# Attention scores: the low queries' product with 64 rows alone, both components as row tiles, one maximum per component

## The chip, the core and the metric

The kernel runs on one core of a Trainium2 chip. The core has a matrix engine (TensorE, PE, with weight loads listed as PEld), three engines for elementwise work (VectorE or DVE, ScalarE or ACT, GpSimd or POOL), a queue that issues DMAs (SyncE, SP), an on-chip memory of 128 partitions, and PSUM, the memory into which PE writes, in 8 banks of 512 fp32 columns. Each engine takes its instructions in the order of the program and waits for the others by semaphores. The metric is the device time of one execution in microseconds (us).

## What is computed

One layer of a backbone with two branches on 1024 latent tokens and 256 context tokens, of width 1024: gated linear attention, and differential attention with 8 heads. The change lies in the differential attention. Its core in the reference:

```python
def diff_attention(q1, q2, k1, k2, v, lam):
    ...
    def one_block(qs):
        qb1, qb2 = qs
        s1 = jnp.einsum('bhqd,bhkd->bhqk', qb1, k1).astype(jnp.float32) * scale
        s2 = jnp.einsum('bhqd,bhkd->bhqk', qb2, k2).astype(jnp.float32) * scale
        a = jax.nn.softmax(s1, axis=-1) - lam * jax.nn.softmax(s2, axis=-1)
        return jnp.einsum('bhqk,bhkv->bhqv', a.astype(v.dtype), v)
```

Each head has two components (q1 with k1, q2 with k2) of 64 channels. Every block of 128 queries is scored against 1280 keys (256 of the context, 1024 latent), in both components; each gets a softmax, and their difference multiplies the values.

## The kernel before

**Numbers in two parts.** Matrix products run on fp32r operands, each value split into a high part and a low part (the rest). A product of two values is made of high x high, high x low and low x high. For the scores, where a component has only 64 channels, the kernel stacks the parts on the 128 rows: the key tile `K[comp]` holds the high part of the keys on rows 0-63 and the low part on rows 64-127 (`att_keys`, L1746 and L1747), and the query tile `Q[comp]` holds the same query part on both halves of the rows, `Q[comp][:, 0]` the high one, `Q[comp][:, 1]` the low one. A score bank is thus two products: j = 0 gives high queries x (high + low keys), j = 1 gives low queries x (high + low keys).

**A unit.** `att_scores` walks over 8 heads and 8 query tiles of 128: 64 units. The scores of a unit, 2 x 1280 columns, fill five PSUM banks side by side (`s5`). Banks 0 and 1 hold 1024 columns of component 0 (MAIN), banks 3 and 4 those of component 1, and bank 2 holds the last 256 columns of component 0 beside the first 256 of component 1 (TAIL). A unit makes 8 products of 512 columns (2 components x 2 banks x j) and 4 of 256 columns. There is one set of these banks: `acq("s0")`, `acq("s1")` and `acq("st")` wait until the exponentials of the unit before have read component 0, component 1, and both.

**What follows a unit.** DVE takes the maximum over component 0's 1024 columns, over the tails of both (one instruction, two results), and over component 1's 1024 columns (`att_max`), and a minimum of two negated maxima for each component (`att_exp`). ACT then makes the exponential of 1280 columns with its sum, for each component. `att_mix` (DVE) joins both components: a reciprocal, a factor, and one pass over 1280 columns. `att_tr` transposes the result on PE, ACT, POOL and DVE split it into two parts (`att_split`), `att_av` multiplies it with the values, and `att_fin` normalises, gates and stores the head's output to `d_bT`.

**The order on each engine.** It is made when the program is built, by a planner (`Driver`): tasks are generators that yield a due time or an event, each instruction gets a modelled cost, and the task with the smallest priority number that is due goes next. The scores have priority 0, the transposes 1, A·V 2, and maxima and exponentials -3. `fill` has priority 9: the projections of the merge gates and of both branches (tiles `mb` while the scores' banks are open, `mc` afterwards), which don't depend on the attention until the branch of the attention itself (`d_bT`) comes up. So fill takes the PE time that the attention leaves, as far as the planner's costs tell it. `mm` (L334) gives the planner the cost of a product; `banked` declares which instructions touch the same banks, so that others don't wait for each other.

Of the kernel before, what the change touches and what calls it, by code (L numbers as in the profile page):

```python
# [13 lines left out]
AF = mybir.ActivationFunctionType  # L14
ALU = mybir.AluOpType
AX = mybir.AxisListType
# [4 lines left out]
P = 128  # L21
# [3 lines left out]
T = S + CTX  # L25
# [203 lines left out]
class Hybrid:  # L229
# [20 lines left out]
        mm=("psA", 3), tp=("psA", 2), edge=("sbE", 1), gs=("psA1", 1), go=("psA1", 1), gt=("psA1", 1),  # L250
# [80 lines left out]
            yield  # L331
        self.d.spawn(later(), AtPE(at), prio=-9)

    def mm(self, out, lhsT, rhs, start, stop, more=False):  # L334
        self.ins = self.nc.tensor.matmul(out, lhsT, rhs, start=start, stop=stop, skip_group_check=more).ins  # L335
        n = rhs.free_size()
        c = 0.009 + max(n, 230) * 0.000428 if rhs.dtype == F32R else 0.006 + max(4 * n, 470) / 2400
        return self.d.op("PE", c, [out], [lhsT, rhs])

# [1387 lines left out]
    def att_keys(self):  # L1727

        for hd in range(8):
            c, x = hd // 4, hd % 4  # L1730
            for i in range(10):
                yield self.ev_st["dk", c, i]
            if hd:
                yield self.ev_q[0, 1]
            else:
                yield self.gla_free[3]
                yield from self.acq("hc", 16)
                Driver.places = (T, 2 * T, 3 * T)
                self.hk = self.t("hk", [P, HK], F32R)
            K = []  # L1740
            for comp in range(2):
                rows = slice(64 * comp, 64 * comp + 64)
                yield from self.acq("kk")
                m = (2 * hd + comp) % 3
                kt = self.hk[:, m * T:(m + 1) * T]
                self.dma(kt[0:64], self.d_kT[0][c][x, rows])  # L1746
                self.dma(kt[64:128], self.d_kT[1][c][x, rows])  # L1747
                K.append(kt)
            self.K[hd] = K
            self.d.set(self.ev_k[hd], self.d.when(*K))  # L1750
# [33 lines left out]
    def att_scores(self):  # L1784

        nc, d = self.nc, self.d
        yield self.ev_b
        s5 = self.t("s5", [P, 2 * T])
        for hd in range(8):
            for qt in range(8):  # L1790
                pr, qs = qt // 2, slice((qt % 2) * P, (qt % 2) * P + P)
                yield self.ev_k[hd]
                yield self.ev_q[hd, pr]
                K, Q = self.K[hd], self.Q[hd, pr]

                def score(po, comp, o, n):
                    bank = po.offset % (2 * T) // 512
                    for j in range(2):
                        e = self.mm(po, Q[comp][:, j, qs], K[comp][:, o:o + n], j == 0, j == 1)
                        self.banked(self.ins, "PE", bank)  # L1800
                    return e

                u = dict(hd=hd, qt=qt, E=[None, None], mt=self.t("sm", [P, 2]), mx=[self.t("sm", [P, 1]) for _ in range(2)],
                         z=self.t("sm", [P, 2]), left=2, ev=[Event() for _ in range(3)])

                for comp in range(2):
                    yield from self.acq(f"s{comp}")
                    pm = s5[:, 1536 * comp:1536 * comp + 1024]
                    for x, (o, n) in enumerate(self.MAIN[comp]):
                        e = score(pm[:, x * 512:(x + 1) * 512], comp, o, n)  # L1810
                        if x == 0:
                            yield AtPE(0)
                    d.spawn(self.att_max(u["ev"][comp], u["mx"][comp], pm, 3 * comp, 3 * comp + 1), On(e, "DVE"), prio=-3)
                    yield AtPE(0)
                    if comp == 0:
                        yield from self.acq("st")
                        pt = s5[:, 1024:1536].rearrange("p (c k) -> p c k", c=2)
                        for x in range(2):
                            e = score(pt[:, x], x, *self.TAIL[x])
                        d.spawn(self.att_max(u["ev"][2], u["mt"], pt, 2), On(e, "DVE"), prio=-3)  # L1820
                    elif qt == 7:
                        self.rel("kk", e, 2)
                    d.spawn(self.att_exp(u, comp, s5), On(e, "DVE"), prio=-3)
                    yield AtPE(0)
                if qt % 2 == 1:
                    self.rel("aq", e, 2)
                d.set(self.ev_u[8 * hd + qt])

    def att_max(self, ev, mx, pm, *banks):
        self.dve.tensor_reduce(mx, pm, AX.X, ALU.max, negate=True)  # L1830
        self.banked(self.dve.ins, "DVE", *banks)
        self.d.set(ev)
        return
        yield

    def att_exp(self, u, comp, s5):
        d, mx = self.d, u["mx"][comp]
        yield u["ev"][2]
        yield u["ev"][comp]
        yield d.on("DVE", mx)  # L1840
        self.dve.tensor_scalar(mx, mx, u["mt"][:, comp:comp + 1], None, ALU.min)
        yield from self.acq("e5")
        E = u["E"][comp] = self.t("e5", [P, T])
        yield d.on("ACT", mx)
        e = self.act.activation(E, s5[:, 1280 * comp:1280 * comp + T], AF.Exp, bias=mx, accum_out=u["z"][:, comp:comp + 1])
        self.banked(self.act.ins, "ACT", *range(2 * comp, 2 * comp + 3))
        self.rel(f"s{comp}", e)
        u["left"] -= 1
        if u["left"] == 0:
            self.rel("st", e)  # L1850
            if (u["hd"], u["qt"]) == (7, 7):
                d.set(self.ev_s2)
            d.spawn(self.att_mix(u), On(e, "DVE"), prio=self.PM)
# [610 lines left out]
```

## Time and profile before

| | us |
|---|---|
| runs, median of 3 | 1687.13 (1684.58, 1687.13, 1691.38) |
| span of the profiled execution, from its first instruction to its last | 1685.9 |
| first score product to last | 911.3 to 1438.6 |
| mean clock granted to PE, as a share of the full one | 0.994 |

The span lies 1.2 us under the median of the runs, and within their spread. In the profile's rows an engine stands ahead of its line, operation and tiles ("out<-in"); tile names lose their numbers, so `s` is the scores' banks `s5`, `hk` the keys, `aq` the queries, `e` the exponentials, `at` the transposed and split weights, `vv` the values, `b` the two banks shared by transposes and A·V, `sm` the small statistics. All products have line L335 (in `mm`), all transposes L361, all elementwise work L197 (in a helper). A row of a group ends with its count, its busy time with the mean length of one in ns, and the idle time of the engine ahead of it with what ended it. A row of the timeline begins with its start and its length in us. A row of the table of stretches gives the stretch, its length, then the busy time and the number of instructions on PE, PEld, DVE, ACT and POOL, the granted clock, the DMA share and GB/s.

### The profile page before, as it was taken

The page shows a single profiled execution, that of the slowest core. Times are in us where ns is not written, and L with a number is a line of the kernel's source. Part 1 is how long each engine was busy: PE and PEld are TensorE (multiplying, and loading weights), DVE is VectorE, ACT ScalarE, POOL GpSimd, SP SyncE. Part 2 cuts the span into 40 slices and gives each one's busy share as a digit, 9 for nine tenths or more (in the row PEclk, how much of TensorE's full clock was granted, in tenths as well). Part 3 has the DMA queues.
Part 4 walks back from the last instruction along what each step waited for, and adds up shares of the span by engine and source line. Part 5 has one row for each costly group of instructions (what it writes and reads, how often), then busy time and mean ns, then how long its engine had stood idle before and what let it go on. Part 6 is the DMA issues. An engine that isn't in the chain of part 4 may idle for free.

```text
span 1685.9 us, 24403 instructions
## 1 busy us (share of the span) xinstructions
PE 1641.8 (97%) x8389; PEld 1358.3 (81%) x8389; DVE 1167.5 (69%) x2035; ACT 788.4 (47%) x1624; POOL 601.7 (36%) x649
## 2 busy tenths in 40 slices
PE   8999999999999999999999999999999999999999
PEld 3788788888788888888878888888888787887887
DVE  4797853455578697687762988787787887525694
ACT  4666423343334535455442665556666555411231
POOL 1500200000156475465530446555565555700000
PEclk9999999999999999999999999999999999999999
DMA  8557947687683665645375344345368552279422
GB/s 305 167 205 258 325 164 248 226 282 273 200 258 114 197 203 169 207 134 169 117 196 154 85 128 132 104 116 138 113 169 245 167 157 67 98 234 337 151 100 75
DMA packets 255884, 302.84 MB, mean 180 GB/s; under 512 B 21480, under 2 KB 173968, under 8 KB 255760
## 3 DMA queue, kind: packets, MB, share of 16 engines
q1 hardware_dynamic: 255760, 301.29, 56.9%
q8 instruction: 66, 1.08, 0.3%
q14 instruction: 58, 0.48, 0.1%
HBM read 203.71 MB, written 97.52 MB: 179 GB/s over the span
## 4 chain that ended last, share of the span: by engine, by line
PE 43%; DVE 6%; ACT 2%; DMA 2%; POOL 2%; issue 2%; ACTq 0%; DVEq 0%; POOLq 0%; SPq 0%
PE mc L335 10%; PE mm L335 7%; PE mb L335 7%; PE s L335 6%; PE b L335 5%; DVE sm L197 3%; PE b L361 3%; POOL at L197 2%; DVE e L197 2%; PE go L335 1%; ACT e L197 1%; DMA h<-d_bT 1%; PE mz L335 1%; PE gs L335 1%; PE tp L361 1%
## 5 line engine op out<-in xcount | busy, mean ns | idle before, releaser
L335 PE MATMUL mm<-w,h 128*128 128x512 f32 x1260 | 319.3, 402 | 0.6 <-DVE w L197 0.4
L335 PEld LDWEIGHTS mm<-w,h 128*128 128x128 f32 x1260 | 232.0, 189 | 48.0 <-issue 1.0
L197 DVE TENSOR_REDUCE sm<-s 128x1 f32<-128x1024 f32 (+1 forms) x192 | 194.4, 1037 | 49.0 <-PE s L335 47.4
L335 PE MATMUL mb<-h,wt 128*128 128x512 f32 x744 | 204.5, 407 | 2.5 <-ACT ft L197 2.1
L197 ACT ACTIVATE e<-s,sm 128x1280 f32<-128x1280 f32 x128 | 169.9, 1330 | 68.0 <-DVE sm L197 60.3
L197 POOL TENSOR_TENSOR at<-ac,at 128x512 fp32r<-128x512 f32 x128 | 184.7, 1443 | 10.7
L197 POOL TENSOR_SCALAR at<-ac 128x512 fp32r<-128x512 f32 x128 | 100.6, 786 | 236.0 <-ACT ac L197 166.9
L335 PE MATMUL s<-hk,aq 128*128 128x512 f32 (+1 forms) x768 | 178.2, 365 | 3.2 <-ACT e L197 1.1
L335 PEld LDWEIGHTS mb<-h,wt 128*128 128x128 f32 x744 | 131.1, 190 | 25.9 <-ACT ft L197 3.6
L335 PE MATMUL mc<-h,wt 128*128 128x512 f32 x600 | 141.2, 392 | 1.7 <-DMA h<-d_bT 0.8
L335 PE MATMUL mm<-h,w 128*128 128x512 f32 x576 | 139.4, 398 | 2.7 <-ACT p L197 1.1
L335 PEld LDWEIGHTS s<-hk,aq 128*128 128x128 f32 x768 | 122.3, 190 | 23.9 <-ACT e L197 5.1
L335 PEld LDWEIGHTS mc<-h,wt 128*128 128x128 f32 x600 | 111.3, 188 | 26.9 <-DMA h<-d_bT 3.3
L335 PE MATMUL b<-at,vv 128*128 128x256 f32 x960 | 130.6, 285 | 0.5 <-POOL at L197 0.4
L335 PEld LDWEIGHTS mm<-h,w 128*128 128x128 f32 x576 | 108.6, 191 | 27.0 <-DVE h L197 1.4
L335 PEld LDWEIGHTS b<-at,vv 128*128 128x128 f32 x960 | 122.7, 190 | 5.6 <-POOL at L197 1.2
L197 POOL TENSOR_TENSOR sm<-sm,nhalf 128x2 f32<-128x2 f32 (+2 forms) x94 | 106.1, 1129 | 53.6 <-DVE sm L197 48.1
L197 DVE TENSOR_TENSOR w<-raw,w 128x512 fp32r<-128x512 f32 x120 | 92.5, 789 | 31.5 <-ACT w L197 30.3
L197 ACT ACTIVATE ac<-b 128x512 f32<-128x512 f32 x120 | 71.1, 600 | 84.9 <-PE b L361 79.7
L197 DVE SCALAR_TENSOR_TENSOR e<-e,sm,e 128x1280 f32<-128x1280 f32 x64 | 108.7, 1698 | 0.6
L197 ACT ACTIVATE w<-raw 128x512 fp32r<-128x512 f32 x120 | 72.5, 628 | 70.3 <-DVE raw L197 22.8
L361 PE MATMUL b<-ident,e 128*128 128x128 f32 x598 | 92.5, 276 | 12.4 <-DVE at L197 4.3
(283 smaller groups left out, 2832.5 us busy)
## 6 DMA issues: line engine op xcount, KB each, us to landing
raw<-in_w_in SPq DMA_DIRECT2D x63, 512.0 KB, 4.7
g<-d_s SPq DMA_DIRECT2D x32, 640.0 KB, 5.2
aq<-d_qT SPq DMA_DIRECT2D x128, 128.0 KB, 3.4
d_dv<-pl SPq DMA_DIRECT2D x40, 256.0 KB, 2.2
gv<-d_v SPq DMA_DIRECT2D x40, 256.0 KB, 3.2
d_kT<-pl SPq DMA_DIRECT2D x40, 256.0 KB, 3.0
hk<-d_kT SPq DMA_DIRECT2D x32, 320.0 KB, 5.7
vv<-d_dv SPq DMA_DIRECT2D x16, 640.0 KB, 6.2
```

The source lines that it names most:

```text
L197: self.ins = f(out, *args, **kw).ins
L335: self.ins = self.nc.tensor.matmul(out, lhsT, rhs, start=start, stop=stop, skip_group_check=more).ins
L361: self.nc.tensor.transpose(out, src, self.ident[:n, :n])
```

## The change

The low queries (j = 1) of the four MAIN banks are multiplied with the high keys alone, on 64 rows: rows 0-63 for component 0 and rows 64-127 for component 1. For that, component 1's key tile has its halves swapped, so that its high part lies on rows 64-127. The product of low queries and low keys is thus left out there; the tails keep it. The four products of 64 rows stand at the end of a unit, in pairs of the two components, each into its own bank, after all products of 128 rows. Their cost to the planner is that of half the columns (`share=0.5`). One maximum over all 1280 columns of a component takes the place of its two maxima and the minimum; both maxima are issued after the last product of the unit. Component 1's `s1` and `st` are now both acquired ahead of the tails.

```diff
-    def mm(self, out, lhsT, rhs, start, stop, more=False):
+    def mm(self, out, lhsT, rhs, start, stop, more=False, share=1.0):
...
-        n = rhs.free_size()
+        n = rhs.free_size() * share
...
-                self.dma(kt[0:64], self.d_kT[0][c][x, rows])
-                self.dma(kt[64:128], self.d_kT[1][c][x, rows])
+                for j in range(2):
+                    self.dma(kt[64 * j:64 * j + 64], self.d_kT[j ^ comp][c][x, rows])
...
-                def score(po, comp, o, n):
-                    bank = po.offset % (2 * T) // 512
-                    for j in range(2):
-                        e = self.mm(po, Q[comp][:, j, qs], K[comp][:, o:o + n], j == 0, j == 1)
-                        self.banked(self.ins, "PE", bank)
+                def full(po, comp, o, n, j, start, stop):
+                    e = self.mm(po, Q[comp][:, j, qs], K[comp][:, o:o + n], start, stop)
+                    self.banked(self.ins, "PE", po.offset % (2 * T) // 512)
                     return e
+                def half(po, comp, o, n):
+                    r = slice(64 * comp, 64 * comp + 64)
+                    e = self.mm(po, Q[comp][r, 1, qs], K[comp][r, o:o + n], False, True, share=0.5)
+                    self.banked(self.ins, "PE", po.offset % (2 * T) // 512)
+                    return e
...
                 for comp in range(2):
                     yield from self.acq(f"s{comp}")
-                    pm = s5[:, 1536 * comp:1536 * comp + 1024]
-                    for x, (o, n) in enumerate(self.MAIN[comp]):
-                        e = score(pm[:, x * 512:(x + 1) * 512], comp, o, n)
-                        if x == 0:
-                            yield AtPE(0)
-                    d.spawn(self.att_max(u["ev"][comp], u["mx"][comp], pm, 3 * comp, 3 * comp + 1), On(e, "DVE"), prio=-3)
-                    yield AtPE(0)
+                    if comp:
+                        yield from self.acq("st")
+                        for x in range(2):
+                            pt = s5[:, 1024 + 256 * x:1280 + 256 * x]
+                            for j in range(2):
+                                full(pt, x, *self.TAIL[x], j, j == 0, j == 1)
+                    for a in main[comp]:
+                        full(*a, 0, True, False)
                     if comp == 0:
-                        yield from self.acq("st")
-                        pt = s5[:, 1024:1536].rearrange("p (c k) -> p c k", c=2)
-                        for x in range(2):
-                            e = score(pt[:, x], x, *self.TAIL[x])
-                        d.spawn(self.att_max(u["ev"][2], u["mt"], pt, 2), On(e, "DVE"), prio=-3)
...
+                        yield AtPE(0)
+                for x in range(2):
+                    for comp in range(2):
+                        e = half(*main[comp][x])
...
+                for comp in range(2):
                     d.spawn(self.att_exp(u, comp, s5), On(e, "DVE"), prio=-3)
...
     def att_exp(self, u, comp, s5):
         d, mx = self.d, u["mx"][comp]
-        yield u["ev"][2]
-        yield u["ev"][comp]
-        yield d.on("DVE", mx)
-        self.dve.tensor_scalar(mx, mx, u["mt"][:, comp:comp + 1], None, ALU.min)
+        pm = s5[:, 1280 * comp:1280 * comp + T]
+        banks = range(2 * comp, 2 * comp + 3)
+        e = self.dve.tensor_reduce(mx, pm, AX.X, ALU.max, negate=True)
+        self.banked(self.dve.ins, "DVE", *banks)
         yield from self.acq("e5")
```

More of the change, by code (lines that the diff above doesn't have):

```diff
@@ L1794, in att_scores @@
                 K, Q = self.K[hd], self.Q[hd, pr]
-                def score(po, comp, o, n):
-                    bank = po.offset % (2 * T) // 512
-                    for j in range(2):
-                        e = self.mm(po, Q[comp][:, j, qs], K[comp][:, o:o + n], j == 0, j == 1)
-                        self.banked(self.ins, "PE", bank)
-                    return e
-                u = dict(hd=hd, qt=qt, E=[None, None], mt=self.t("sm", [P, 2]), mx=[self.t("sm", [P, 1]) for _ in range(2)],
-                         z=self.t("sm", [P, 2]), left=2, ev=[Event() for _ in range(3)])
+                def full(po, comp, o, n, j, start, stop):
+                    e = self.mm(po, Q[comp][:, j, qs], K[comp][:, o:o + n], start, stop)
+                    self.banked(self.ins, "PE", po.offset % (2 * T) // 512)
+                    return e
@@ new lines, in half @@
+                def half(po, comp, o, n):
[3 more added lines that the diff above has]
+                    return e
+                u = dict(hd=hd, qt=qt, E=[None, None], mx=[self.t("sm", [P, 1]) for _ in range(2)], z=self.t("sm", [P, 2]), left=2)
+                main = [[(s5[:, 1536 * c + 512 * x:1536 * c + 512 * x + 512], c, *self.MAIN[c][x]) for x in range(2)]
+                        for c in range(2)]
@@ L1814, in att_scores @@
-                    yield AtPE(0)
-                    if comp == 0:
-                        yield from self.acq("st")
-                        pt = s5[:, 1024:1536].rearrange("p (c k) -> p c k", c=2)
-                        for x in range(2):
-                            e = score(pt[:, x], x, *self.TAIL[x])
-                        d.spawn(self.att_max(u["ev"][2], u["mt"], pt, 2), On(e, "DVE"), prio=-3)
-                    elif qt == 7:
-                        self.rel("kk", e, 2)
+                    if comp:
[4 more added lines that the diff above has]
+                                full(pt, x, *self.TAIL[x], j, j == 0, j == 1)
@@ L1823, in att_scores @@
+                    for a in main[comp]:
+                        full(*a, 0, True, False)
+                    if comp == 0:
+                        yield AtPE(0)
+                for x in range(2):
+                    for comp in range(2):
+                        e = half(*main[comp][x])
+                if qt == 7:
+                    self.rel("kk", e, 2)
+                for comp in range(2):
                     d.spawn(self.att_exp(u, comp, s5), On(e, "DVE"), prio=-3)
-                    yield AtPE(0)
+                yield AtPE(0)
@@ L1827, in att_scores @@
                 d.set(self.ev_u[8 * hd + qt])
[L1829 to L1834, printed above, removed]
     def att_exp(self, u, comp, s5):
         d, mx = self.d, u["mx"][comp]
-        yield u["ev"][2]
-        yield u["ev"][comp]
-        yield d.on("DVE", mx)
-        self.dve.tensor_scalar(mx, mx, u["mt"][:, comp:comp + 1], None, ALU.min)
+        pm = s5[:, 1280 * comp:1280 * comp + T]
+        banks = range(2 * comp, 2 * comp + 3)
+        e = self.dve.tensor_reduce(mx, pm, AX.X, ALU.max, negate=True)
+        self.banked(self.dve.ins, "DVE", *banks)
         yield from self.acq("e5")
@@ L1844, in att_exp @@
         yield d.on("ACT", mx)
-        e = self.act.activation(E, s5[:, 1280 * comp:1280 * comp + T], AF.Exp, bias=mx, accum_out=u["z"][:, comp:comp + 1])
-        self.banked(self.act.ins, "ACT", *range(2 * comp, 2 * comp + 3))
+        e = self.act.activation(E, pm, AF.Exp, bias=mx, accum_out=u["z"][:, comp:comp + 1])
+        self.banked(self.act.ins, "ACT", *banks)
         self.rel(f"s{comp}", e)
```

## The prediction

> **What bounds the kernel now.** I read the page's head first, then the table of stretches for the stage in which the scores run, then who waits for whom there.
>
> ```profile
> span 1685.9 us, 24403 instructions
> PE 1641.8 (97%) x8389; PEld 1358.3 (81%) x8389; DVE 1167.5 (69%) x2035; ACT 788.4 (47%) x1624; POOL 601.7 (36%) x649
> ...
> 911.00:1439.00 528.00, 509.24 (x3038) 433.82 (x3039) 425.86 (x806) 314.11 (x634) 285.92 (x262) 0.99 0.47 133
> ...
> PE b L361 <- DVE at L197: 4.3, 6, 1.6
> PEld s L335 <- ACT e L197: 5.1, 12, 0.9
> PE s L335 <- ACT e L197: 1.1, 3, 0.5
> ```
>
> TensorE (PE) is busy 97% of the span, and 509.24 of 528 us in the stage from the first score product to the last; DVE has 425.86 there. The last three rows (waiting engine, line, releaser; total us, times, longest) are from the waits in that stage: the scores wait for the exponential of the unit before for 5.1 + 1.1 = 6.2 us in all. So a microsecond of PE work taken away is worth one, unless PE then waits. A microsecond of DVE work is worth nothing by itself.
>
> **PE work taken away.** The stage has 64 units (8 heads x 8 query tiles) of 12 score products.
>
> ```profile
> L335 PE MATMUL s<-hk,aq 128*128 128x512 f32 x512 | 144.7, 402 | 2.1 <-ACT e L197 1.1 <-ACT p L197 0.7
> L335 PE MATMUL s<-hk,aq 128*128 128x256 f32 x256 | 43.7, 292 | 1.1 <-DMA hk<-d_kT 0.7
> 1499.63 12.63 PE L335 MATMUL mc<-h,wt 128*128 128x512 f32 x55
> 526.11 1.89 PE L335 MATMUL gs<-gqr,gkk 128*128 128x64 f32 x16
> 527.81 1.39 PE L335 MATMUL mm<-w,h 128*128 128x512 f32 x5
> ```
>
> The price of one product is its spacing, not its own length, since they are pipelined. In the run of 55 (third row, from the timeline), one lasts 0.389 us, so the spacing is (12.63 - 0.389) / 54 = 0.2267 us. Of 512 products with 512 columns, 256 (four in each unit) become products of 64 rows, in pairs: rows 0-63 for one component, rows 64-127 for the other, into different banks. Their number stays the same.
>
> If the two of a pair run side by side, a pair takes the time of one, 0.2267 us instead of 0.4534: two pairs in a unit, 64 x 2 x 0.2267 = 29.0 us saved. If they don't, nothing is saved. No row of this trace shows two products side by side, so 0 and 29.0 are the ends. What could stand between is the weight load that each product has: 16 products of only 64 columns (fourth row) take 527.81 - 526.11 = 1.70 us, 0.106 each, so two loads take 0.212, less than 0.2267, and don't stop a pair. If the second of a pair lags by one such load, a unit loses 0.106 once: 64 x (0.4534 - 0.106) = 22.2. I take the middle of 22.2 and 29.0, **-25.6 us**; the row that bears on it, the weight load, is nearest to this end. The Trainium skill (TensorE: Matmul & The Clock Gate, Part 3, Measured speedup vs the span model) gives 3.07 times for four row tiles of 32 rows. By the same share of the ideal a pair would run 1.54 times as fast, an estimate that would make this term 20.3 us; no run here shows it yet.
>
> **Going into and out of the row tiles.** Each unit changes from 128-row products to 64-row ones and back, 128 changes in all. The nearest rows are products with few weight columns, and some with 4 rows, between full ones:
>
> ```profile
> 36.37 2.88 PE L335 MATMUL mm<-h,w 128*128 128x512 f32 x12
> 39.08 0.63 PE L335 MATMUL gs<-pl,cs 128*2 128x512 f32 x2
> ...
> 40.94 1.55 PE L335 MATMUL mm<-h,w 128*128 128x512 f32 x6
> 42.33 0.62 PE L335 MATMUL gs<-pl,cs 128*2 128x512 f32 x2
> ...
> 46.56 0.40 PE L361 MATMUL gt<-ident,p 4*128 4x4 f32 x4 [0.67 <-DVE p L197]
> 46.90 1.09 PE L361 MATMUL tp<-ident,g 128*128 128x128 f32 x8
> ```
>
> From 36.37 to 42.33 there are 26 products of 512 columns (8 of them with 2 or 4 weight columns) and three changes of shape: 5.96 us against 26 x 0.2267 = 5.89, 0.02 us a change. After the four small transposes, of which one lasts 0.20, the last starts at 46.76 and the next full one 0.14 later, where full ones follow each other every (1.09 - 0.27) / 7 = 0.117: 0.03 us. The ends are 0 and a complete drain, where the next product starts at the end of the one before: 0.389 - 0.227 = 0.162, 128 x 0.162 = 20.7 us. I take 0.03, from the rows that change the number of rows: **+3.8 us**. The Trainium skill (TensorEngine Tiling (Array Packing), Key Properties) says that changing the tiling mode drains the TensorE. By that the term would be the 20.7 of the upper end. The rows with few weight columns don't show such a drain (0.02 us); for 64-row tiles no run here shows it.
>
> **DVE.** Per unit two maxima over 1024, one over two times 256, and two minima become two maxima over 1280.
>
> ```profile
> L197 DVE TENSOR_REDUCE sm<-s 128x1 f32<-128x1024 f32 x128 | 155.6, 1216 | 48.4 <-PE s L335 46.8 <-ACT e L197 1.3 <-PE b L361 0.3
> L197 DVE TENSOR_REDUCE sm<-s 128x2 f32<-128x512 f32 x64 | 43.6, 681 | 0.6 <-PE s L335 0.6
> L197 DVE TENSOR_SCALAR sm<-sm,sm x192: 195/203/216, 915.4 to 1481.4; 128x1 f32<-128x1 f32 x192
> L197 DVE RECIPROCAL sm<-sm x64: 146/155/165, 918.5 to 1447.2; 128x1 f32<-128x1 f32 x64
> L197 DVE TENSOR_SCALAR sm<-sm,sm,nlam x64: 272/273/276, 918.7 to 1447.4; 128x1 f32<-128x1 f32 x64
> L197 DVE SCALAR_TENSOR_TENSOR e<-e,sm,e x64: 1540/1550/2550, 920.1 to 1447.7; 128x1280 f32<-128x1280 f32 x64
> ```
>
> By the first two rows 512 more elements cost 0.535 us, so 1280 take 1.216 + 0.267 = 1.48. A unit goes from 2 x 1.216 + 0.681 + 2 x 0.203 = 3.52 to 2.96 us, 36 us less over the stage. I cost that at nothing: PE sets the stage and waits for DVE only now and then.
>
> **The wait that is added.** Before, component 0 of a unit could be reduced while PE made component 1. Now both maxima begin only after the last half product, and the unit's tails and component 1's full products wait until both exponentials of the unit before are read (before, the tails had that wait as well, but component 0's maximum was already running). PE takes its instructions in order: behind the waiting score product stand the projections (mb), the transposes and A·V (b), and ACT, POOL and DVE wait for those. How long the chain is, from one unit to the next:
>
> ```profile
> 912.55 2.95 DVE L197 TENSOR_REDUCE sm<-s 128x1 f32<-128x1024 f32 x3 [30.20 <-PE s L335]
> ...
> 951.71 1.32 ACT L197 ACTIVATE e<-s,sm 128x1280 f32<-128x1280 f32 x1
> 952.92 0.20 ACT L197 ACTIVATION_READ_ACCUMULATOR e<-s,sm 128x1 f32 x1
> ...
> 951.62 0.19 ACT L197 ACTIVATION_READ_ACCUMULATOR e<-s,sm 128x1 f32 x1
> 951.86 2.51 PE L335 MATMUL s<-hk,aq 128*128 128x512 f32 x10 [0.28 <-ACT e L197]
> ```
>
> Three reductions in a row take 2.95 us where their lengths add up to 3.11, so each overlaps its neighbour by 0.08: two of 1280 take 2.88, the first alone 1.48. An exponential with its read takes 953.12 - 951.71 = 1.41. A wait costs some 0.05 (the read ends at 951.81, the product starts at 951.86). From the start of the last half product: 0.39 + 0.05 + 1.48 + 0.05 + 1.41 + 0.05 = 3.43 us until component 0's banks are free, and 0.39 + 0.05 + 2.88 + 0.05 + 1.41 + 0.05 = 4.83 until component 1's are. Less the 0.23 that PE spends on that last product, other PE work must fill 3.2 and 4.6 us.
>
> In the program order of the changed kernel I counted the PE work between these places (0.227, 0.119 and 0.117 us for 512, 256 and 128 columns, from the rows above and, for 256, 2.15 us / 18 = 0.119 of A·V). Its median is 4.0 and 5.8 us, so most units cover it, but a few don't: unit 34 has 1.42 us ahead of component 0 and 2.34 up to the tails, unit 2 has 1.62 and 2.30, unit 62 has 1.83 and 4.13. The shortfalls, each unit's taken after the stall it has had, add up to 9.6 us in 9 of 63 units. And DVE isn't free: in 56 of 64 units it has the mix of the unit before (0.155 + 0.273 + 1.55 = 1.98 us, begun when the second exponential is read) ahead of the maxima, while PE, if it goes on at once, needs 4 x 0.119 + 2 x 0.227 + 2 x 0.227 + 0.2 = 1.6: 0.4 later, needs of 3.6 and 5.0, and 14.5 us of shortfall. With two smaller DVE operations of 0.4 in front as well it is needs of 4.4 and 5.8, and 39.2. I take 14.5, and the old 6.2 us go: **+8.3 us**, from -6.2 (all covered) to +33.0.
>
> ```profile
> 1192.56 2.15 PE b L335 x18
> L197 DVE TENSOR_TENSOR at<-b,at 128x256 fp32r<-128x256 f32 x59 | 24.6, 417 | 23.1 <-ACT at L197 22.9
> ```
>
> **Edits at nothing.** The key loads are as many and as large as before; component 1 only has its two halves swapped. The order puts 72 more projection products (72 x 0.2267 = 16.3 us) ahead of the last score and as many fewer behind it: moved, not saved. The first product that needs the last head's output stands 24.5 us of PE work behind that head's last transpose (39.5 before), and a store of this kind lands in 3.0 and a load in 5.7 us, so that cover holds:
>
> ```profile
> d_kT<-pl SPq DMA_DIRECT2D x40, 256.0 KB, 3.0
> hk<-d_kT SPq DMA_DIRECT2D x32, 320.0 KB, 5.7
> ```
>
> **The sum.** -25.6 + 3.8 + 8.3 = -13.5 on a span of 1685.9 gives 1672.4; the median of the runs (1687.13) lies 1.2 above that span, so **1673.6 us**, 0.8% faster. 0.5%, or 8.4 us, is about what a measurement can tell from no change.
>
> **The rivals.**
> - *A drain at each change of tile height.* 20.7 in place of 3.8: 1690.5, no change to be told. If the next weights are loaded only after the drain as well (0.188 us each, by the row below), 128 x 0.35 = 44.8: 1714.6. For it: no row has 64-row tiles. Against it: the 0.02 and 0.03 us above.
>
> ```profile
> L335 PEld LDWEIGHTS s<-hk,aq x768: 186/188/331, 911.3 to 1438.3; 128*128 128x128 f32 x192
> ```
>
> - *The score chain becomes the bound (slower).* In every unit the two maxima now come one behind the other after all products, with DVE's other work before them. At needs of 4.4 and 5.8 us the shortfall is 39.2: 1673.6 + 24.7 = 1698.3. It decides from 14.5 + 13.5 = 28 us on (0.44 a unit) and is slower by over 0.5% from 36.4. For it: median cover (4.0, 5.8) is no more than that need. Against it: DVE has 36 us less to do, and the mix alone gives 14.5.
> - *The pairs don't overlap*, the change doesn't do what it says: 1673.6 + 25.6 = 1699.2. For it: no row shows overlap. Against it: different rows, different banks, and a weight load that leaves room.
> - *Better than the sum*: 29.0 saved, no price for the changes, 9.6 of shortfall: 1687.1 - 29.0 + 3.4 = 1661.5.
>
> **How the numbers follow.** My forecast 0.55 (own range 1662 to 1681, of it 0.50 faster by over 0.5%), better 0.05, drain 0.15 (0.10 no change, 0.05 slower), chain 0.13 (0.09 slower), no overlap 0.12 (0.10 slower). That is faster 0.55, same 0.21, slower 0.24. The range is 1659 to 1700: it holds the better case, the plain drain, the chain and the case without overlap, and leaves out the drain with exposed weights and the far ends.
>
> **What would show it.** Pairs: the four half products of a unit take about 0.48 us from first to last start plus one spacing; at 0.9 the overlap is wrong. Changes: the gap around them, against 0.227. The chain: the waits of score products for ACT, forecast at some 14 us in the stage against 6.2, and idle time of PE. The maxima: 1.48 us each, 128 of them. If PE's work from the first to the last score falls by less than 10 us after the 16.3 us of moved projections are taken out, the first term is wrong; if it falls by 20 or more and the time doesn't, the stalls are.

## The result and the profile after

| | before | after |
|---|---|---|
| median of the runs, us | 1686.66 (1684.58 to 1691.38, 4 runs) | 1728.15 (1727.09 to 1729.67, 4 runs) |
| ratio, 95% interval | | 1.024 [1.0225, 1.0256] |
| span of the profiled execution, us | 1685.9 | 1728.0 |

The changed kernel is 2.4% slower; the forecast was 0.8% faster, with a range up to 1700. First the head of its page, the stretch from the first score product to the last, and the longest waits of score products in that stretch (waiting engine, line, releaser: total us, times, longest):

```profile
span 1728.0 us, 24202 instructions
PE 1649.9 (95%) x8389; PEld 1328.1 (77%) x8389; DVE 1147.5 (66%) x1843; ACT 786.3 (46%) x1624; POOL 618.8 (36%) x649
```

```profile
911.00:1495.00 584.00, 532.62 (x3106) 416.81 (x3108) 410.33 (x621) 314.33 (x636) 304.45 (x262) 0.98 0.43 125
```

```profile
PEld s L335 <- ACT e L197: 52.1, 49, 3.5
...
PE s L335 <- ACT e L197: 36.3, 40, 3.2
...
PEld s L335 <- issue: 24.0, 65, 0.7
```

The span is 42.1 us longer. Score products waited 1.1 us for ACT's exponentials before and wait 36.3 us now: that is most of it. DVE is less busy (1167.5 to 1147.5 us, 20 us of the forecast 36), and it helps nobody. The last row is new: ahead of the first half product of each of the 64 units the weight load stands still for 0.37 us without waiting for anything that the profile names. PE is busy 8 us longer, although 128 products' worth of time should have gone.

The groups of the score products, with their idle time, and the new maxima (the same line in the groups as before's two rows):

```profile
L335 PE MATMUL s<-hk,aq 128*128 128x512 f32 x256 | 87.2, 423 | 34.6 <-ACT e L197 33.9 <-ACT p L197 0.7
L335 PE MATMUL s<-hk,aq 64*128 64x512 f32 x256 | 47.4, 448 | 0.0
L335 PE MATMUL s<-hk,aq 128*128 128x256 f32 x256 | 44.9, 298 | 2.6 <-ACT e L197 2.4
...
L197 DVE TENSOR_REDUCE sm<-s 128x1 f32<-128x1280 f32 x128 | 184.9, 1483 | 61.8 <-PE s L335 60.2
```

The maximum takes the 1.48 us that were worked out. The wait sits in front of the 128-row products of 512 columns, the first ones that component 0's banks are needed for. One unit of the changed kernel, on DVE, ACT, PE and in the weight loads (timeline: start, length; the rows with x1 on PE are from narrow windows, and the first of them is the last full product ahead of the half ones):

```profile
1006.60 1.54 DVE L197 SCALAR_TENSOR_TENSOR e<-e,sm,e 128x1280 f32<-128x1280 f32 x1
1008.06 2.88 DVE L197 TENSOR_REDUCE sm<-s 128x1 f32<-128x1280 f32 x2
```

```profile
1010.97 1.33 ACT L197 ACTIVATE e<-s,sm 128x1280 f32<-128x1280 f32 x1 [4.37 <-DVE sm L197]
1012.20 0.19 ACT L197 ACTIVATION_READ_ACCUMULATOR e<-s,sm 128x1 f32 x1
1012.29 1.32 ACT L197 ACTIVATE e<-s,sm 128x1280 f32<-128x1280 f32 x1
1013.50 0.20 ACT L197 ACTIVATION_READ_ACCUMULATOR e<-s,sm 128x1 f32 x1
```

```profile
1006.73 0.40 PE L335 MATMUL s<-hk,aq 128*128 128x512 f32 x1
1007.05 0.50 PE L335 MATMUL s<-hk,aq 64*128 64x512 f32 x2
1007.39 0.40 PE L335 MATMUL s<-hk,aq 64*128 64x512 f32 x2
1007.71 0.39 PE L335 MATMUL b<-at,vv 128*128 128x256 f32 x1
...
1012.44 0.73 PE L335 MATMUL s<-hk,aq 128*128 128x512 f32 x2 [0.45 <-ACT e L197]
...
1013.75 1.88 PE L335 MATMUL s<-hk,aq 128*128 128x256 f32 x10
```

```profile
1005.89 0.79 PEld L335 LDWEIGHTS s<-hk,aq 128*128 128x128 f32 x6 [0.15 <-ACT e L197]
1007.05 0.30 PEld L335 LDWEIGHTS s<-hk,aq 64*128 64x128 f32 x4 [0.37 <-issue]
1007.71 2.20 PEld L335 LDWEIGHTS b<-at,vv 128*128 128x128 f32 x18 [0.36 <-issue]
```

Two things stand in these rows.

*The exponential of component 0 is late.* Its own maximum ends 1.48 us after 1008.06, at 1009.54, but it starts at 1010.97, just after both maxima (1010.94), on an ACT that had been idle for 4.37 us. Over the trace it starts after component 1's maximum in 63 of 64 units. In the code both touch bank 2: component 0's maximum and exponential cover banks 0, 1, 2 and component 1's banks 2, 3, 4, and `banked` orders instructions of different engines on one bank. From the start of the last half products (1007.39) to the end of the exponential's read it takes 5.0 us for component 0 and 6.3 for component 1, where the prediction had 3.4 and 4.8. PE resumes 0.05 us after each read.

*The pairs do run side by side, and each change of height has a price.* Two half products start together at 1007.05, two at 1007.39. But ahead of the first weight load of 64 rows and ahead of the next of 128 rows the load engine stands for 0.37 and 0.36 us, and each of these loads starts together with its product, not ahead of it. From the last full product on, the starts lie 0.32, 0.34 and 0.32 us apart, where full products follow each other every 0.227.

### The profile page after: what moved, and what is told of

Its sections match the earlier page's. It is cut to its first block, busy times and chain, and to the rows that moved or that the text cites. A ratio compares the mean times of both kernels' runs of the same rounds, so it can differ in the third digit from the quotient of the medians.

```text
span 1728.0 us, 24202 instructions
## 1 busy us (share of the span) xinstructions
PE 1649.9 (95%) x8389; PEld 1328.1 (77%) x8389; DVE 1147.5 (66%) x1843; ACT 786.3 (46%) x1624; POOL 618.8 (36%) x649
## 4 chain that ended last, share of the span: by engine, by line
PE 36%; DVE 11%; ACT 6%; issue 3%; DMA 2%; POOL 0%; SPq 0%; ACTq 0%; DVEq 0%; POOLq 0%
PE mc L335 9%; DVE sm L197 8%; PE mm L335 7%; PE s L335 6%; PE mb L335 5%; ACT e L197 4%; PE b L335 3%; DVE e L197 2%; PE b L361 2%; PE go L335 1%; PE mz L335 1%; DMA h<-d_bT 1%; PE gs L335 1%; PE tp L361 1%; PE gt L335 1%
## 5 line engine op out<-in xcount | busy, mean ns | idle before, releaser
L197 DVE TENSOR_REDUCE sm<-s 128x1 f32<-128x1280 f32 x128 | 184.9, 1483 | 61.8 <-PE s L335 60.2
L335 PE MATMUL mb<-h,wt 128*128 128x512 f32 x816 | 222.7, 407 | 3.2 <-ACT ft L197 2.2
L197 POOL TENSOR_SCALAR at<-ac 128x512 fp32r<-128x512 f32 x128 | 114.4, 894 | 276.3 <-ACT ac L197 257.9
L335 PE MATMUL s<-hk,aq 128*128 128x512 f32 (+2 forms) x768 | 161.8, 390 | 37.2 <-ACT e L197 36.3
L335 PEld LDWEIGHTS mb<-h,wt 128*128 128x128 f32 x816 | 144.1, 190 | 30.9 <-ACT ft L197 3.4
L335 PEld LDWEIGHTS s<-hk,aq 128*128 128x128 f32 (+1 forms) x768 | 94.2, 193 | 81.4 <-ACT e L197 52.1
L335 PE MATMUL mc<-h,wt 128*128 128x512 f32 x528 | 123.7, 392 | 1.3 <-DMA h<-d_bT 0.5
L335 PEld LDWEIGHTS mc<-h,wt 128*128 128x128 f32 x528 | 98.1, 188 | 24.4 <-DMA h<-d_bT 2.6
```

Source lines behind the costliest of these rows:

```text
L197: self.ins = f(out, *args, **kw).ins
```

## The experiments

Every kernel ran three rounds against the kernel before on the same chip; ratios are to that. "Score waits" are the waits of score products for ACT's exponentials, before the weight load and before the product, which overlap: 5.1 and 1.1 us in the kernel before, 52.1 and 36.3 in the changed one.

**e1_full_rows: the row tiles undone.**

```diff
-                    e = self.mm(po, Q[comp][r, 1, qs], K[comp][r, o:o + n], False, True, share=0.5)
+                    e = self.mm(po, Q[comp][:, 1, qs], K[comp][:, o:o + n], False, True)
```

> The changed kernel with the low queries' products on all 128 rows again (low queries x low keys included, planner's cost that of a full product): order, one maximum per component and the added wait stay, the row tiles go. Theory: the added time is the chain of the scores (component 0's exponential waits for both maxima, because component 1's maximum shares bank 2 with it; waits of score products for ACT 36.3 us against 6.2), and the row tiles are worth about nothing (four half products with both changes of height cost 0.88 us against 0.91 for four full ones): 1722 to 1736 us, waits for ACT above 25 us. Rival: the row tiles themselves cost the time: about 1687 us, near the kernel before.

1766.5 us, 1.0456 [1.0434, 1.0478], score waits 64.9 and 48.1. The tiles aren't what costs, but the forecast missed by 30 us to the other side. The products' cost to the planner had changed as well, and with it the whole order (768 instead of 816 products of the fill in `mb`). e8_full_same_plan takes this apart.

**e2_three_max: row tiles with the old maxima.**

```diff
+                        d.spawn(self.att_max(u["ev"][2], u["mt"], pt, 2), On(e, "DVE"), prio=-3)
...
+                    d.spawn(self.att_max(u["ev"][comp], u["mx"][comp], pm, 3 * comp, 3 * comp + 1), On(e, "DVE"), prio=-3)
```

> The changed kernel with its row tiles and its order of products, but with the three maxima and the two minima of the kernel before (the tails' maximum issued right after the tails; component 1's own maximum touches banks 3 and 4 alone). Theory (exponential 0 waits for maximum 1 through bank 2): exponential 0 starts before maximum 1 ends, waits of score products for ACT under 15 us, 1688 to 1705 us. Rival (the tiles cost the time): stays at 1720 or more. Rival (all products of a unit before its maxima, whatever the banks): 1710 or more.

1690.79 us, 1.002 [1.0006, 1.0033], score waits 11.6 and 4.2. The time is as forecast, but not the reason: the exponential of component 0 still started after all three maxima, in all 64 units, since the planner puts the minima behind them. So a late exponential need not cost, and this run doesn't tell the bank from the planner.

**e3_planner_told and e12_told_wait_only: the planner learns of the wait.** The instructions are those of the changed kernel. In e12 the planner is told only that component 0's exponential is ready after both maxima; e3 has the cost of a half product raised to a full one's as well (`share=1.0`).

```diff
+        if comp:
+            d.set(u["both"])
+        yield u["both"]
+        k0, k1 = d.key(u["mx"][0]), d.key(u["mx"][1])
+        d.ready[k0] = max(d.ready[k0], d.ready[k1])
```

> The changed kernel with the same instructions, but the planner is told what the trace shows: exponential 0 is ready only after both maxima, and a half product costs as much as a full one (0.22 us, changes of height included). Theory: the chain is longer than PE's other work only because that work is placed elsewhere; told, the planner puts more projections between the units: waits of score products for ACT under 15 us, 1685 to 1702 us. Rival: the chain of a unit is too long however it is planned (or the projections run out): 1715 us or more.

> The changed kernel with the same instructions and the same planner's costs (a half product at half cost); the planner is told only that component 0's exponential is ready after both maxima, not after its own. Theory (PE stalls because the planner counts on component 0's banks 1.4 us too early; the length of the chain as such is covered by projections once it is known): waits of score products for ACT fall from 36 us to under 12, time 1685 to 1703 us. Rival (the cost of the half products was what misled it in e3_planner_told): 1715 us or more.

e3: 1698.28 us, 1.0058 [1.0039, 1.0078], score waits 4.0 and 1.4. e12: 1695.8 us, 1.0046 [1.003, 1.0063]: 32 us less than the changed kernel, from the order alone. The exponential is as late as ever, and PE has work until then. The waits of e12 by the tile `s`, and one unit on PE and ACT:

```profile
PEld s L335: 10.5, 19
...
PE s L335: 4.1, 8
```

```profile
1005.80 3.70 PE L335 MATMUL mb<-h,wt 128*128 128x512 f32 x15
1009.34 0.60 PE L361 MATMUL b<-ident,e 128*128 128x128 f32 x4
1009.70 0.95 PE L335 MATMUL mb<-h,wt 128*128 128x512 f32 x3
1010.48 0.63 PE L335 MATMUL s<-hk,aq 128*128 128x512 f32 x2
```

```profile
1008.41 1.33 ACT L197 ACTIVATE e<-s,sm 128x1280 f32<-128x1280 f32 x1 [1.65 <-DVE sm L197]
1009.64 0.19 ACT L197 ACTIVATION_READ_ACCUMULATOR e<-s,sm 128x1 f32 x1
```

Fifteen products of the fill, four transposes and three more products stand where PE used to wait; the scores come 0.65 us after the read, not 0.05. (The two rows of waits say who waited for the tiles `s`: engine, tile, line; us, times.)

**e13_own_banks: the shared bank taken away, the planner told nothing.** Component 0 keeps its one maximum; component 1 gets one over its tail in bank 2, early, one over banks 3 and 4, and a minimum.

```diff
+        self.dve.tensor_reduce(u["mt"], pt, AX.X, ALU.max, negate=True)
+        self.banked(self.dve.ins, "DVE", 2)
...
-        e = self.dve.tensor_reduce(mx, pm, AX.X, ALU.max, negate=True)
-        self.banked(self.dve.ins, "DVE", *banks)
+        e = self.dve.tensor_reduce(mx, s5[:, 1536:2560] if comp else pm, AX.X, ALU.max, negate=True)
+        self.banked(self.dve.ins, "DVE", *((3, 4) if comp else banks))
```

> The changed kernel with the shared bank taken out of component 1's maximum, the planner told nothing: component 0 keeps its one maximum over 1280 columns (banks 0, 1, 2); component 1 has a maximum over its tail (256 columns of bank 2, issued after the tails), one over its 1024 columns (banks 3, 4) and a minimum. Theory (exponential 0 waits for maximum 1 because both touch bank 2): it now starts some 0.1 us after its own maximum and before maximum 1 ends, last score start to the read of exponential 0 takes 3.4 to 3.9 us instead of 4.8, waits of score products for ACT fall to under 15 us, time 1685 to 1703 us. Rival (the bank isn't the reason: ACT or DVE is late anyway, or the chain is too long with both maxima after all products): exponential 0 still starts after maximum 1, time 1715 us or more.

1690.65 us, 1.0022 [1.0009, 1.0035], score waits 11.0 and 7.4. One unit on DVE and ACT:

```profile
1006.30 0.42 DVE L197 TENSOR_REDUCE sm<-s 128x1 f32<-128x256 f32 x1
1006.88 2.62 DVE L197 TENSOR_REDUCE sm<-s 128x1 f32<-128x1280 f32 x2 [0.15 <-PE s L335]
```

```profile
1008.40 1.33 ACT L197 ACTIVATE e<-s,sm 128x1280 f32<-128x1280 f32 x1
1009.63 0.19 ACT L197 ACTIVATION_READ_ACCUMULATOR e<-s,sm 128x1 f32 x1
```

The row of two maxima is the one over 1280 (1006.88 to 1008.36) and the one over banks 3 and 4 (to 1009.50). The exponential starts at 1008.40, right after its own and 1.1 us before the other ends. That holds in 61 of 64 units, and last score start to the read of exponential 0 takes 3.6 us in the median, against 4.8 in the changed kernel. 37 us of the time are gone, with the planner told of no wait. It made a new order for the new instructions, though (792 products of the fill in `mb` instead of 816), so the 37 us hold what that order is worth as well; the next section sets the runs side by side.

**e6_before_bank2 and e10_three_max_bank2: the bank counted in where it wasn't.** The kernel before, and e2_three_max, with component 1's maximum declared on bank 2 too.

```diff
-                    d.spawn(self.att_max(u["ev"][comp], u["mx"][comp], pm, 3 * comp, 3 * comp + 1), On(e, "DVE"), prio=-3)
+                    d.spawn(self.att_max(u["ev"][comp], u["mx"][comp], pm, *((2, 3, 4) if comp else (0, 1))), On(e, "DVE"), prio=-3)
```

> The kernel before with one thing declared: component 1's maximum over banks 3 and 4 counts as touching bank 2 as well, so that component 0's exponential waits for it, or it for the exponential, whichever was issued first. Instructions and planner's costs are those of the kernel before. Theory (this dependence, which the planner doesn't know, is what stalls PE): waits of score products for ACT rise from 6 to over 25 us and the time to 1705 to 1735 us. Rival (the dependence is harmless; what costs is that both maxima begin only after all products): 1684 to 1695 us.

> The kernel e2_three_max with component 1's maximum declared to touch bank 2 as well, as in the changed kernel; order on every engine and planner as in e2_three_max. Theory (the wait through bank 2 costs only where the planner counts on an earlier exponential; in e2_three_max it places the minima, and with them the exponentials, behind all three maxima anyway): 1687 to 1698 us. Rival (that wait by itself is the loss): 1710 us or more.

e6: 1698.54 us, 1.0071 [1.0053, 1.0088], score waits 9.8 and 5.6; slower by 11 us, less than forecast: in the old order component 0's exponential came after component 1's maximum in 52 of 64 units anyway (60 here). e10: 1691.68 us, 1.0019 [1.0009, 1.003], within 1 us of e2_three_max. The wait costs what the plan has not covered, not its own length.

**e7_three_max_told against e9_three_max_full: what the row tiles are worth.** Both have three maxima and a half product costed in full, and the same order on PE, DVE, ACT and POOL (a few DMAs swap places); e9 has the products on 128 rows.

```diff
-                    e = self.mm(po, Q[comp][r, 1, qs], K[comp][r, o:o + n], False, True, share=1.0)
+                    e = self.mm(po, Q[comp][:, 1, qs], K[comp][:, o:o + n], False, True, share=1.0)
```

> The kernel with row tiles and three maxima (run e2_three_max), with a half product costed to the planner as a full one (0.22 us with its share of the changes of height). Theory: PE then does what the planner expects, the remaining waits of score products for ACT (4 us on the products, 12 us on their weight loads) shrink, and the time is 1680 to 1691 us. Rival: the remaining waits have nothing to do with the planned cost, same time as e2_three_max within 3 us.

> The same kernel as e7_three_max_told, instruction by instruction on every engine, but the low queries' products have all 128 rows. Where no chain waits, the difference is what the row tiles are worth. Theory (two changes of height at 0.21 us take back what the two pairs save, 0.45 us a unit): 0.88 against 0.91 us a unit, so 0 to +6 us against e7_three_max_told. Rival (a change costs 0.03 us as forecast): +25 us.

e7: 1692.26 us, 1.0028 [1.0017, 1.0039], no better than e2_three_max and just outside its forecast. e9: 1695.0 us, 1.0046 [1.0031, 1.0061]. Where hardly a score waits (under 1 us on the products in both), the row tiles are worth **2.7 us**, 0.04 a unit; the two intervals touch, so it may be nothing. The weight loads at the same place of both, e7 first:

```profile
1005.32 0.79 PEld L335 LDWEIGHTS s<-hk,aq 128*128 128x128 f32 x6
1006.48 0.30 PEld L335 LDWEIGHTS s<-hk,aq 64*128 64x128 f32 x4 [0.36 <-issue]
1007.15 0.42 PEld L361 LDWEIGHTS b<-ident,e 128*128 128x128 f32 x4 [0.37 <-issue]
1007.53 0.77 PEld L335 LDWEIGHTS b<-at,vv 128*128 128x128 f32 x6
```

```profile
1004.01 1.72 PEld L335 LDWEIGHTS s<-hk,aq 128*128 128x128 f32 x10
1005.77 0.59 PEld L361 LDWEIGHTS b<-ident,e 128*128 128x128 f32 x4
1006.33 0.77 PEld L335 LDWEIGHTS b<-at,vv 128*128 128x128 f32 x6
```

From the first tail's load to A·V's, e7 takes 2.21 us and e9 2.32. Two pairs save 0.45, so the two changes cost 0.34 in this unit, and 0.45 - 0.04 = 0.41 by the time: 0.17 to 0.21 a change. Four half products' loads take 0.30 in place of four times 0.12, so they overlap as well.

**e4_four_changes: twice the changes of height.** The first pair is made before component 1's second full product.

```diff
+                        if comp:
+                            for b in range(2):
+                                e = half(*main[b][x])
```

> The changed kernel with its two pairs apart: the first pair before component 1's second full product, the second after it, so that a unit changes the height of the rows four times, not twice. Same products. Theory (a change costs 0.21 us, because the array drains and the next weights are loaded only then): 64 x 2 x 0.21 = 27 us more work on PE, of which the waits of the score products (36 us) can hide a part: 1733 to 1755 us, idle weight loads that wait for nothing ahead of score products twice as many (about 128 against 64). Rival (a change costs 0.03 us or nothing, and the pairs don't overlap): 1726 to 1732 us.

1752.31 us, 1.038 [1.0363, 1.0397]: 24 us over the changed kernel. PE is busy 1678.2 us against 1649.9, 28.3 us for 128 more changes, 0.22 each, of which the score waits hide 4 (36.3 to 32.1). The granted clock was 0.987 against 0.990, by estimate 5 us over the span, so 0.22 is an upper figure (0.18 without them). The idle loads ahead of score products that wait for nothing are 192, not 128, since three of the four changes lead to a score product. One unit's loads:

```profile
1007.26 0.19 PEld L335 LDWEIGHTS s<-hk,aq 64*128 64x128 f32 x2 [0.26 <-issue]
1007.69 0.19 PEld L335 LDWEIGHTS s<-hk,aq 128*128 128x128 f32 x1 [0.24 <-issue]
1008.13 0.18 PEld L335 LDWEIGHTS s<-hk,aq 64*128 64x128 f32 x2 [0.25 <-issue]
1008.56 2.21 PEld L335 LDWEIGHTS b<-at,vv 128*128 128x128 f32 x18 [0.24 <-issue]
```

A stop at each of the four changes, and 0.43 to 0.44 us from one to the next, whether one pair or one full product of 0.227 lies between: a pair takes the time of one product, and a change some 0.21.

**e8_full_same_plan: the changed kernel's order, full rows.** The order is the same on PE, DVE, ACT and POOL; two DMAs swap places.

```diff
-                    e = self.mm(po, Q[comp][r, 1, qs], K[comp][r, o:o + n], False, True, share=0.5)
+                    e = self.mm(po, Q[comp][:, 1, qs], K[comp][:, o:o + n], False, True, share=0.5)
```

> The changed kernel with the low queries' products on all 128 rows and the planner's cost left as it is (half), so that the order on every engine is exactly that of the changed kernel. Theory: where the chain waits, only the change into the half products and the pairs lie on it, not the change out of them: 0.45 + 0.21 = 0.66 us become 0.91 on the chain, up to 64 x 0.24 = 16 us more: 1730 to 1746 us, and the further time of e1_full_rows (1766) came from its other plan. Rival (the row tiles are worth more than that, 0.43 us a unit or more): 1755 us or more.

1732.31 us, 1.0267 [1.0248, 1.0286]: 4 us over the changed kernel, at the low end. So also where scores wait the tiles are worth a few us at most (the intervals of the two kernels touch), and 34 us of e1_full_rows came from its order alone.

**e5_no_pairs: the half products by component.**

```diff
-                for x in range(2):
-                    for comp in range(2):
+                for comp in range(2):
+                    for x in range(2):
```

> The changed kernel with the four half products in the order component 0, component 0, component 1, component 1 instead of by pairs of both components; the same products, two changes of height a unit, the planner's costs the same. Theory (two half products on different rows run side by side, two on the same rows don't): the group takes 3 x 0.227 instead of 2 x 0.227 us, 0.227 a unit on PE and on the chain of the scores, up to 14.5 us: 1736 to 1744 us, and the next weight load comes 0.88 us after the group's first one instead of 0.66. Rival (no overlap, the short group has another reason): 1728 us, no change.

1747.9 us, 1.0346 [1.0319, 1.0373], but not for the forecast reason: from the group's first load to the next of 128 rows it takes 0.67 us, against 0.66 in the changed kernel.

```profile
1010.14 0.30 PEld L335 LDWEIGHTS s<-hk,aq 64*128 64x128 f32 x4 [0.36 <-issue]
1010.81 0.20 PEld L361 LDWEIGHTS b<-ident,b1k 128*128 128x128 f32 x2 [0.37 <-issue]
```

The group is as short in either order, and the trace tells why. Of the four half products, the second and the fourth in this program signal DVE when they end. In the trace the two that start first (0.007 us apart) signal nothing and the two that start 0.34 us later do, in all 64 units. So component 1's first half product starts ahead of component 0's second, out of the program's order, and the pairs form although they aren't adjacent in the program. The 20 us go with another order (840 products of the fill in `mb` instead of 816), with score waits of 69.3 and 51.6.

**e11_three_max_075: an attempt at a better version.** e2_three_max with `share=0.75`.

> A version that might beat both: e2_three_max with a half product costed at 0.75 of a full one (0.17 us), between e2_three_max and e7_three_max_told; the instructions are the same. By the theory the row tiles are worth 0 to 3 us where no chain waits, so 1684 to 1694 us, not clear of the kernel before. Rival (the rest of the stalls comes from this cost): under 1682 us.

1703.82 us, 1.0089 [1.0069, 1.011]: outside its forecast, and slower than with 0.5 or 1.0. No version that was run beats the kernel before.

## Why the prediction was wrong

- **PE work taken away: right in kind, the size near the better end.** The half products run side by side. The term was -25.6 of at most -29.0; in e4_four_changes a pair takes the time of one full product, so 29.0 is the better figure.
- **Going into and out of the row tiles: mis-sized, and it took the gain back.** The term was +3.8 (0.03 us a change). Measured are 0.45 - 0.04 = 0.41 us a unit, 26.3 us in all. The rows chosen, few weight columns and 4-row transposes, did not stand in for a change of 64 rows. The rival named for it, a complete drain (20.7) with the next weights loaded only afterwards (up to 44.8), fits, and the measured price lies between its two: the first load after a change starts only together with its product. The Trainium skill (TensorEngine Tiling (Array Packing), Key Properties) says that a change of tiling mode drains the array, and for these 64-row tiles the trace agrees: 0.17 to 0.22 us each.
- **The wait that is added: this is the step that failed.** It put component 0's exponential right after its own maximum (3.43 us from the last half product to free banks, 4.83 for component 1). The runs show it after both maxima, through the bank that the one maximum over 1280 columns now shares: 4.8 and 6.5 us in the median. With needs of 3.6 and 5.0 us the count of uncovered time gave 14.5 us; PE's waits for the exponentials at score products were 36.3, near the 39.2 that the same count gave for needs of 4.4 and 5.8 (measured, less the 0.23 of the last product: 4.6 and 6.3). So the count held up and the needs were wrong: where e13_own_banks takes the sharing away, component 0's read comes after 3.6 us (component 1's after 5.8, with its added minimum), and PE waits 7.4. The old waits in this term were misread too: the 5.1 us of the weight loads and the 1.1 of the products overlap, so of the 6.2 us PE itself lost 1.1. To 36.3 that is 35.2 more, where the term should have read 14.5 - 1.1 = 13.4. `banked` and the bank numbers in the diff would have told it: maximum 1 over banks 2 to 4, exponential 0 over banks 0 to 2.
- **How far the runs bear this out.** In the new order of products, the five kernels in which exponential 0 waits for maximum 1 through bank 2 and the planner counts on it earlier (the changed one, e1, e4, e5, e8) took 1728 to 1767 us. The eight in which the wait is absent, told, or covered because the plan has the exponential late anyway (e2, e3, e7, e9 to e13) took 1691 to 1704. e12 keeps the wait and e13 takes it away; both bring back over 30 us. Their orders differ from the changed kernel's: within the five the order alone is worth 34 us (e1 and e8), within the eight up to 13. So the wait through the bank is the cause, while the 37.5 us between the changed kernel and e13 also hold what their orders differ by.
- **The rival "the score chain becomes the bound" was the right one**, for a reason that it didn't name. Its point of 28 us of waits was passed, and the 36.4 for a clear loss was reached to within 0.1: 36.3. Its own time, 1698.3, fell short by 30 us, in part because it had the changes of height at 3.8. But it is not a bound: the same chain, known to the planner, costs little (e12_told_wait_only).
- **Edits at nothing: right.** DVE's saving did not show in the time, and no load of the keys or of `d_bT` came into the way (PE waited 0.5 us for `d_bT`, 0.8 before).
- **The signs that it named.** PE's busy time from the first to the last score, less the 16.3 us of moved projections, rose by 532.62 - 509.24 - 16.3 = 7.1 us, where under 10 us less was to mean that the first term is wrong. It can't mean that: the figure also holds the changes of height (26.3) and a lower clock (0.98 against 0.99). The half products took 0.34 us from the first to the last start, 0.57 with one spacing, nearer the 0.48 of an overlap than the 0.9 without.
- **The sum, put right:** 1673.6, with 3.4 more saved by the pairs, 26.3 - 3.8 = 22.5 more for the changes and 13.4 - 8.3 = 5.1 more for the old waits, is 1697.8. Where the bank is not shared (e13_own_banks), PE's waits rose by 7.4 - 1.1 = 6.3 in place of 13.4, which gives 1690.7, and 1690.65 were measured; so close an agreement is partly luck, as plans differ by more. For the changed kernel the measured 35.2 in place of 13.4 give 1719.6, which leaves 8.5 of the 1728.15 unexplained.

Open is how much of this is the granted clock: over the whole span it was 0.990 against 0.994, by estimate 17 against 10 us of clock lost, about the 8.5. No run held it fixed, but e12_told_wait_only had the same 0.990 and took 32 us less, so those 32 are not the clock's.

## What to carry to other kernels

Before merging two operations over PSUM, write down the banks of the merged one: an instruction that reaches one bank further can order itself behind an engine that it had nothing to do with. A planner that doesn't know such a wait places everything else wrongly, and the loss is the uncovered time rather than the wait: tell it, or remove the shared bank. Row tiles pay by the number of tiles run between two changes of mode: here two pairs saved 0.45 us and two changes cost 0.41.

## What the hardware showed that was not expected

- A change between 128-row and 64-row products costs 0.17 to 0.22 us each way, while one between 128 weight columns and 2 or 4 had cost 0.02 in the trace of before.
- Half products on different rows start together (1007.05 twice, 1007.39 twice) whichever of them stand side by side in the program; in e5_no_pairs, with both of one component first, component 1's first started ahead of component 0's second in all 64 units, and the group took 0.67 us against 0.66. For these row tiles the order on PE is not simply that of the program.
- Two orders of the same instructions differed by 34 us (e1_full_rows and e8_full_same_plan), and three planned costs of one product gave 1691, 1704 and 1692 us (0.5, 0.75 and 1.0 of a full one). A difference of 10 us between two plans is no evidence on the instructions.
